# Attention sublayer of an encoder layer: gate and half of the second modulation summed in 1024-column pieces, in tiles of their own

## Chip, cores and metric

One core of one Trainium2 chip runs the whole layer as one program. The metric is the device time of one execution in microseconds (us); lower is better. PE is the matrix engine, PEld its weight loads, DVE the vector engine, ACT the scalar engine, POOL the general engine, SP the engine that here only issues DMAs. SPq is SP's queue of DMA issues, which runs in order.

## What is computed

One layer for a sequence of 512 rows of 2048 float32 values:

```python
mod = silu(c) @ w_ada + b_ada                     # 2048 x 12288 weights
sh1, sc1, gt1, sh2, sc2, gt2 = split(mod, 6)
h = rms_norm(x) * (1 + sc1) + sh1
mix = [differential attention(h), latent attention(h)] @ w_out
x = x + gt1 * mix
h2 = rms_norm(x) * (1 + sc2) + sh2
x = x + gt2 * ((silu(h2 @ w_gate) * (h2 @ w_up)) @ w_down)
```

Both attentions have 8 heads. c is one vector, so `silu(c) @ w_ada` is a vector times a matrix of 2048 rows. Those weights are read once and are not worth a matmul; DVE sums the products.

## The kernel before

**Matmuls.** float32 operands are split into a high part (ACT rounds, `hi`) and a low part (DVE or POOL subtracts, `lo`), and each product is three PE passes (`mm3`, lines 242 to 244). Class `Weights` loads a weight chunk into one of three `raw` tiles (lines 74 and 78, on SP), splits it (lines 90 and 98) and keeps two chunks ahead.

**A modulation sum.** `ada_sum` (line 299) sets 128 partitions to 16 rows of c each. For every q of the 16 it loads 128 rows by `width` columns of `w_ada` (line 308, SP) and DVE does acc = raw * c_col[q] + acc (line 315; the first one of a sum without a bias is a plain multiply, line 312). With a bias (line 303 and 304) POOL first clears acc and SP loads the bias into its first row. After 16 such steps the 128 partial rows are added up on PE by a product with ones. `ada_pair` (line 326) does the same for two parts at once: one tile holds `n` columns of the shift and `n` of the scale.

**Order of the work.** Only PE runs in the order in which the program is written. The order on each other engine is planned when the program is built, from its dependencies. In the attention the program is written as two hand-made lists of steps, one for a head of differential attention (`DIFF_STEPS`, nine `F`) and one for latent attention (`MLA_STEPS`, eight `F`, four of them `F1`). At each `F`, `between(us, n)` puts in `us` of projection matmuls as filler (`DIFF_FILL` and `MLA_FILL` per head; only 0.2 us for the fourth latent head) and then `n` steps of the generator `side_work`. `n` comes from `DIFF_SIDE[head]` and from `MLA_SIDE[0]` or `[1]`.

**Side work.** `side_work` first runs `gate1`: the 2048 columns of gt1, 512 at a time, by `ada_row` (line 359): 16 steps of one load and one sum, a step with the split of the sum (ACT and DVE), and a step with two matmuls by ones, a row copied out by DVE (line 953) and written to DRAM (line 954). That is 18 steps for each of 4 blocks. When the latent heads begin, `second_modulation` sums shift and scale of h2 for the first 8 of 16 column tiles (`MOD_EARLY`), 512 columns at a time by `ada_sums`: 32 sum steps, 6 empty ones and one with `ada_columns` (line 346, 16 small matmuls, line 354, and three DVE operations, lines 355 to 357) for each of 2 blocks. The other 8 column tiles are done later, in the output projection, and gt2 in the last stage; both by the same functions with other tiles.

**Tiles.** All loads and sums of the side work take slots of one ring `A` of 45 tiles of 512 columns (`slot_of`), which also holds the normed input, the latents, latent-attention keys and the attention's outputs. DMA scratch takes 16 KB of each partition in the build's default.

Of the kernel before, what the change touches and what calls it, by code (L numbers as in the profile page):

```python
# [10 lines left out]
F32 = mybir.dt.float32  # L11
F32R = mybir.dt.float32r
AF = mybir.ActivationFunctionType
ALU = mybir.AluOpType
# [4 lines left out]
P = 128  # L19
D = 2048  # L20
# [179 lines left out]
def hybrid_layer(ctx, tc, a, out):  # L200
    nc = tc.nc
    act, dve, pool, pe, sp = nc.scalar, nc.vector, nc.gpsimd, nc.tensor, nc.sync
# [9 lines left out]
    def open_pool(name, side="left"):  # L212
        p = tc.tile_pool(name=name, bufs=1, reuse_waits="tile", side=side)
        return p, p.__enter__()
# [8 lines left out]
    def slot(name, dt=F32R):  # L223
        return big.tile([P, S], dt, tag="A", bufs=N_SLOTS, name=name)

    def bank(tag, name):
        return psum.tile([P, 512], F32, tag=tag, name=name)

    turn, spare = [0], ["tmp"]

    def next_tag():
        turn[0] ^= 1
        return "tmp" if turn[0] else "acc"

    def f(ap):
        return ap.bitcast(F32)
# [17 lines left out]
    ones_r = const.tile([P, P], F32R, name="ones_r")  # L254
# [44 lines left out]
    def ada_sum(raws, accs, col0, width, nq, bias=None):  # L299

        acc = accs()
        if bias is not None:
            pool.memset(acc[:, :width], 0.0)
            sp.dma_start(out=acc[0:1, :width], in_=bias)
        for j in range(KC // nq):
            raw = raws()
            raw = raw[:, :nq * width].rearrange("p (q n) -> p q n", q=nq)
            sp.dma_start(out=raw, in_=w_ada[:, nq * j:nq * (j + 1), col0:col0 + width])
            for i in range(nq):
                q = nq * j + i  # L310
                if bias is None and q == 0:
                    dve.tensor_scalar(out=acc[:, :width], in0=raw[:, i, :width], scalar1=c_col[:, 0:1], scalar2=None,
                                      op0=ALU.mult)
                else:
                    dve.scalar_tensor_tensor(out=acc[:, :width], in0=raw[:, i, :width], scalar=c_col[:, q:q + 1],
                                             in1=acc[:, :width], op0=ALU.mult, op1=ALU.add)
            yield None
        yield acc

    def ada_sums(raws, accs, p_scale, p_shift, k0, nk, nq, sums):  # L320
        for part in (p_scale, p_shift):
            acc = None
            for acc in ada_sum(raws, accs, part * D + k0 * P, nk * P, nq):
                if acc is None:
                    yield None
            sums.append(acc)
# [21 lines left out]
    def ada_columns(sums, k0, nk, G, SH, cg, cbs, cbh):  # L348

        ks = slice(k0, k0 + nk)  # L350
        ps = bank(spare[0], "ps_ada")
        for i, acc in enumerate(sums):
            for m in range(nk):
                pe.matmul(ps[:, i * nk + m:i * nk + m + 1], acc[:, tsl(m)], ones, start=True, stop=True)
        dve.tensor_tensor(out=G[:, ks], in0=ps[:, 0:nk], in1=scol(cbs + k0, nk), op=ALU.add)
        dve.tensor_tensor(out=G[:, ks], in0=G[:, ks], in1=scol(cg + k0, nk), op=ALU.mult)
        dve.tensor_tensor(out=SH[:, ks], in0=ps[:, nk:2 * nk], in1=scol(cbh + k0, nk), op=ALU.add)

    def ada_row(raws, accs, part, c0, width, nq, tag, emit):

        acc = None
        col0 = part * D + c0
        for acc in ada_sum(raws, accs, col0, width, nq, b_ada[0:1, col0:col0 + width]):
            if acc is None:
                yield None
        ah, al = accs(F32R), accs(F32R)
        act.copy(out=ah[:, :width], in_=acc[:, :width])
        dve.tensor_tensor(out=al[:, :width], in0=acc[:, :width], in1=f(ah)[:, :width], op=ALU.subtract)
        yield None
        ps = bank(tag or spare[0], "ps_row")  # L370
        pe.matmul(ps[:, :width], ones_r, ah[:, :width], start=True, stop=False)
        pe.matmul(ps[:, :width], ones_r, al[:, :width], start=False, stop=True)
        emit(ps[:, :width], c0, width)
        yield None


    def raws0():
# [50 lines left out]
    ps = bank("tmp", "ps_small")  # L428
# [43 lines left out]
    k0, nk, _, _ = MODULATE[0]  # L472
# [112 lines left out]
    for i, (k0, nk) in enumerate(BLOCKS):  # L585
        final = i + 1 == len(BLOCKS)
        for h in range(1 if final else FIRST):
            tag = next_tag()
# [20 lines left out]
    wk = open_pool("wk")  # L609
# [337 lines left out]
    def slot_of(dt=F32):  # L947
        return slot("ada", dt)

    def gate1():  # L950
        def emit(ps, c0, width):
            row = slot_of()
            dve.tensor_copy(out=row[0:1, :width], in_=ps[0:1, :])
            sp.dma_start(out=rowd[0:1, c0:c0 + width], in_=row[0:1, :width])

        for c0 in range(0, D, 512):
            yield from ada_row(slot_of, slot_of, 2, c0, 512, 1, "tmp", emit)

    def out_half(b):

# [9 lines left out]
    def second_modulation(raws, accs, k0, k1, nq):  # L970
        for k in range(k0, k1, 4):
            sums = []
            yield from ada_sums(raws, accs, 4, 3, k, 4, nq, sums)
            for _ in range(6):
                yield None
            ada_columns(sums, k, 4, G2, SH2, C_G2, C_BSC2, C_BSH2)
            yield None
            G2_done[0] = k // 4 + 1
# [20 lines left out]
    def side_work():  # L999
        if GATE_EARLY:  # L1000
            yield from gate1()
        while 0 not in started:
            yield None
        if not GATE_EARLY:
            yield from gate1()
        yield from second_modulation(slot_of, slot_of, 0, MOD_EARLY, 1)

    half, G2_done = {}, [0]
    spare[0] = "tmp"
# [3 lines left out]
    def between(us, n):  # L1013
        fill.run(us)
        for _ in range(n):
            next(side, None)
# [9 lines left out]
    for h in range(H):  # L1026
        cur = diffs[h]
        for step in DIFF_STEPS.split():
            kind, i = step[0], int(step[1:] or 0)
            if kind == "F":  # L1030
                between(DIFF_FILL[h] / DIFF_STEPS.count("F"), DIFF_SIDE[h])
            elif kind == "n":
# [17 lines left out]
    for g in range(H + 1):  # L1050
# [4 lines left out]
        for step in MLA_STEPS.split():  # L1055
            kind, i = step[0], int(step[1:] or 0)
            if kind == "F":
                if g < H:
                    between(MLA_FILL[g] / MLA_STEPS.count("F"), MLA_SIDE[i])
            elif kind == "o":  # L1060
# [52 lines left out]
    def accs2(dt=F32):  # L1113
        return xtile("adaacc", dt)

    mod2 = second_modulation(xtile, accs2, MOD_EARLY, KC, 1)
    turn[0] = 1
    due = 0.0
    for b in range(4):
        tag = next_tag()  # L1120
# [265 lines left out]
    for u in range(N_UNITS):  # L1386
# [4 lines left out]
        else:  # L1391
# [4 lines left out]
                         in_=ao.rearrange("p (f c) s -> p f (c s)", f=2))  # L1396
# [3 lines left out]
    sums = [[fd[1].tile([P, 512], F32, tag="sums", bufs=16, name="sums") for _ in range(4)] for _ in range(NT)]  # L1400
# [26 lines left out]
    for i, n in enumerate(PARTS):  # L1427
        for b in range(4):
            tag = next_tag()
# [43 lines left out]
START_FILL = 5.2  # L1473
DIFF_STEPS = "s0 F s1 n F t0 F e s2 v0 F t1 F s3 v1 F t2 F o0 v2 t3 F o1 v3 F"
DIFF_FILL = (26.0, 26.0, 26.0, 26.0, 26.0, 26.0, 26.0, 26.3)
DIFF_SIDE = (1, 2, 1, 2, 1, 2, 1, 1)
MLA_SIDE = (1, 2)
MOD_EARLY = 8
MOD_PACE = (2.0, 2.4, 2.7, 1.5)
MLA_STEPS = "s0 F t0 e F1 t1 s1 v0 F t2 F1 v1 t3 s2 F v2 F1 o0 v3 F o2 o3 s3 o1 F1"  # L1480
# [39 lines left out]
```

## Time and profile before

| | us |
|---|---|
| three runs, median (lowest to highest) | 2257.24 (2250.57 to 2259.51) |
| profiled execution | 2254.27 |
| its span, first to last instruction | 2252.5 |
| granted TensorE clock, mean | 0.996 |

The profile lists how long each engine was busy, what it waited for, and which instructions it ran. Its windows give the busy time of each engine in a stretch of the span. The differential heads run from about 200 to 530 us, the latent ones from about 540 to 750 us; then come the output projection and, from about 890 us on, the feed-forward part.

### The profile page before, as it was taken

The page shows a single profiled execution, that of the slowest core. Times are in us where ns is not written, and L with a number is a line of the kernel's source. Part 1 is how long each engine was busy: PE and PEld are TensorE (multiplying, and loading weights), DVE is VectorE, ACT ScalarE, POOL GpSimd, SP SyncE. Part 2 cuts the span into 40 slices and gives each one's busy share as a digit, 9 for nine tenths or more (in the row PEclk, how much of TensorE's full clock was granted, in tenths as well). Part 3 has the DMA queues.
Part 4 walks back from the last instruction along what each step waited for, and adds up shares of the span by engine and source line. Part 5 has one row for each costly group of instructions (what it writes and reads, how often), then busy time and mean ns, then how long its engine had stood idle before and what let it go on. Part 6 is the DMA issues. An engine that isn't in the chain of part 4 may idle for free.

```text
span 2252.5 us, 35369 instructions
## 1 busy us (share of the span) xinstructions
PE 2178.6 (97%) x13906; PEld 2000.5 (89%) x13906; DVE 1648.1 (73%) x2362; ACT 942.6 (42%) x1567; POOL 262.7 (12%) x408
## 2 busy tenths in 40 slices
PE   3899999998989999999999999999999999999999
PEld 3899998998777788899999999999999888888887
DVE  5997888868988687867777777777777677443554
ACT  4434555566555334534444444444444522221221
POOL 0003444345554000000000000000000000000000
PEclk9999999999999999999999999999999999999999
DMA  9995355422442684523333333333334686333443
GB/s 284 302 292 169 83 154 158 134 87 86 158 139 96 247 295 159 159 85 118 117 118 117 132 122 122 114 118 116 122 123 131 219 296 224 99 127 99 154 149 103
DMA packets 270826, 345.00 MB, mean 153 GB/s; under 512 B 15005, under 2 KB 171142, under 8 KB 270530
## 3 DMA queue, kind: packets, MB, share of 16 engines
q1 hardware_dynamic: 267864, 338.18, 46.5%
q10 hardware_dynamic: 2794, 4.55, 0.5%
q8 instruction: 109, 1.79, 0.3%
q14 instruction: 59, 0.48, 0.1%
HBM read 322.71 MB, written 19.96 MB: 152 GB/s over the span
## 4 chain that ended last, share of the span: by engine, by line
PE 67%; DVE 1%; DMA 0%; ACT 0%; issue 0%; POOL 0%; SPq 0%; DVEq 0%
PE ps_d L243 7%; PE ps_d L244 7%; PE ps_d L242 7%; PE ps_X L1285 5%; PE ps_X L1283 5%; PE ps_X L1284 5%; PE ps_W L1285 3%; PE ps_W L1283 3%; PE ps_W L1284 3%; PE ps_Y L1285 2%; PE ps_Z L1285 2%; PE ps_o L242 2%; PE ps_o L244 2%; PE ps_o L243 2%; PE ps_Y L1283 2%; PE ps_Z L1283 2%
## 5 line engine op out<-in xcount | busy, mean ns | idle before, releaser
L90 ACT CAST hi<-raw 128x1024 fp32r<-128x1024 f32 (+2 forms) x228 | 221.2, 970 | 479.2 <-PE ps_d L243 262.7
L98 DVE TENSOR_TENSOR lo<-raw,hi 128x1024 fp32r<-128x1024 f32 (+2 forms) x215 | 242.6, 1129 | 217.3 <-ACT hi L90 213.5
L1266 ACT CAST wh<-wr 128x1024 fp32r<-128x1024 f32 x160 | 168.2, 1051 | 245.3 <-PE ps_X L1284 69.2
L1285 PE MATMUL ps_X<-comb,wl 128*128 128x256 f32 x960 | 269.4, 281 | 0.0
L1283 PE MATMUL ps_X<-comb,wh 128*128 128x256 f32 x960 | 268.6, 280 | 0.0
L1284 PE MATMUL ps_X<-comb,wh 128*128 128x256 f32 x960 | 267.1, 278 | 0.0
L1249 DVE TENSOR_TENSOR wl<-wr,wh 128x1024 fp32r<-128x1024 f32 x160 | 195.6, 1222 | 76.5 <-ACT wh L1266 76.2
L244 PE MATMUL ps_d<-lo,ax 128*128 128x512 f32 x640 | 249.0, 389 | 0.0
L243 PE MATMUL ps_d<-hi,ax 128*128 128x512 f32 x640 | 249.0, 389 | 0.0
L242 PE MATMUL ps_d<-hi,ax 128*128 128x512 f32 x640 | 249.0, 389 | 0.0
L242 PE MATMUL ps_in<-hi,hh 128*128 128x384 f32 (+2 forms) x704 | 234.9, 334 | 3.3 <-ACT hh L397 1.3
L243 PE MATMUL ps_in<-hi,hl 128*128 128x384 f32 (+2 forms) x704 | 229.2, 326 | 4.3 <-DVE hl L403 4.3
L244 PE MATMUL ps_in<-lo,hh 128*128 128x384 f32 (+2 forms) x704 | 229.2, 326 | 3.4 <-DVE lo L98 3.4
L1266 ACT CAST wh<-wt 128x1024 fp32r<-128x1024 f32 x120 | 126.4, 1053 | 196.0 <-PE ps_X L1284 118.5
L1249 DVE TENSOR_TENSOR wl<-wt,wh 128x1024 fp32r<-128x1024 f32 x120 | 146.7, 1223 | 80.5 <-ACT wh L1266 80.3
L1283 PEld LDWEIGHTS ps_X<-comb,wh 128*128 128x128 f32 x960 | 180.5, 188 | 0.0
L1284 PEld LDWEIGHTS ps_X<-comb,wh 128*128 128x128 f32 x960 | 180.5, 188 | 0.0
L1285 PEld LDWEIGHTS ps_X<-comb,wl 128*128 128x128 f32 x960 | 180.2, 188 | 0.0
L1285 PE MATMUL ps_W<-comb,wl 128*128 128x256 f32 x640 | 179.6, 281 | 0.0
L1283 PE MATMUL ps_W<-comb,wh 128*128 128x256 f32 x640 | 179.2, 280 | 0.0
L1284 PE MATMUL ps_W<-comb,wh 128*128 128x256 f32 x640 | 178.1, 278 | 0.0
L242 PEld LDWEIGHTS ps_d<-hi,ax 128*128 128x128 f32 x640 | 120.2, 188 | 25.0
(324 smaller groups left out, 5330.6 us busy)
## 6 DMA issues: line engine op xcount, KB each, us to landing
raw<-in_w_down_dram SPq DMA_DIRECT2D x88, 512.0 KB
araw<-in_w_ada_dram SPq DMA_DIRECT2D x80, 512.0 KB
wr<-in_w_gate_dram SPq DMA_DIRECT2D x40, 1024.0 KB
wr<-in_w_up_dram SPq DMA_DIRECT2D x40, 1024.0 KB
ada<-in_w_ada_dram SPq DMA_DIRECT2D x128, 256.0 KB
raw<-in_w_in_dram SPq DMA_DIRECT2D x128, 192.0 KB
raw<-in_w_out_dram SPq DMA_DIRECT2D x32, 512.0 KB
x<-in_w_ada_dram SPq DMA_DIRECT2D x64, 256.0 KB
```

The costliest lines, as they stand in the source:

```text
L90: nc.scalar.copy(out=hi[:, :n], in_=raw[:, :n])
L98: e.tensor_tensor(out=lo[:, :n], in0=raw[:, :n], in1=hi[:, :n].bitcast(F32), op=ALU.subtract)
L242: pe.matmul(o, ah, bh, start=start, stop=False)
L243: pe.matmul(o, al, bh, start=False, stop=False)
L244: pe.matmul(o, ah, bl, start=False, stop=stop)
L1249: dve.tensor_tensor(out=out, in0=x, in1=y, op=ALU.subtract)
L1266: act.copy(out=hi, in_=src)
L1283: pe.matmul(ps[bk], wh[:, k], c[:, 0], start=first and k == 0, stop=False, skip_group_check=True)
L1284: pe.matmul(ps[bk], wh[:, k], c[:, 1], start=False, stop=False, skip_group_check=True)
L1285: pe.matmul(ps[bk], wl[:, k], c[:, 0], start=False, stop=k == 7, skip_group_check=True)
```

## The change

gt1 is now summed 1024 columns at a time (2 blocks of 16 sums instead of 4) and the early second modulation with `ada_pair`, 512 columns of each of the two parts in one tile (2 blocks of 16 sums instead of 32). The loads go to two new tiles `sraw` and the sums to one new tile `sacc`, of 1024 columns each, in the attention's own pool. `ada_row` splits its sum 512 columns at a time; for the gate the split parts and the row stay slots of ring `A`. The steps at each `F` become one everywhere, none in the last differential head. The DMA scratch is set to 1 KB, which makes room for the 12 KB of new tiles.

```diff
-    def ada_row(raws, accs, part, c0, width, nq, tag, emit):
+    def ada_row(raws, accs, part, c0, width, nq, tag, emit, halves=None):
...
-        ah, al = accs(F32R), accs(F32R)
-        act.copy(out=ah[:, :width], in_=acc[:, :width])
-        dve.tensor_tensor(out=al[:, :width], in0=acc[:, :width], in1=f(ah)[:, :width], op=ALU.subtract)
-        yield None
-        ps = bank(tag or spare[0], "ps_row")
-        pe.matmul(ps[:, :width], ones_r, ah[:, :width], start=True, stop=False)
-        pe.matmul(ps[:, :width], ones_r, al[:, :width], start=False, stop=True)
-        emit(ps[:, :width], c0, width)
-        yield None
+        for i in range(0, width, 512):
+            part = acc[:, i:i + 512]
+            ah, al = [(halves or accs)(F32R)[:, :512] for _ in range(2)]
+            act.copy(out=ah, in_=part)
+            dve.tensor_tensor(out=al, in0=part, in1=f(ah), op=ALU.subtract)
+            yield None
+            ps = bank(tag or spare[0], "ps_row")
+            pe.matmul(ps, ones_r, ah, start=True, stop=False)
+            pe.matmul(ps, ones_r, al, start=False, stop=True)
+            emit(ps, c0 + i, 512)
+            yield None
...
+    def side_raw():
+        return wk[1].tile([P, 1024], F32, tag="sraw", bufs=2, name="sraw")
+
+    def side_acc():
+        return wk[1].tile([P, 1024], F32, tag="sacc", bufs=1, name="sacc")
...
-        for c0 in range(0, D, 512):
-            yield from ada_row(slot_of, slot_of, 2, c0, 512, 1, "tmp", emit)
+        for c0 in range(0, D, 1024):
+            yield from ada_row(side_raw, side_acc, 2, c0, 1024, 1, "tmp", emit, slot_of)
...
-            yield from ada_sums(raws, accs, 4, 3, k, 4, nq, sums)
+            if raws is side_raw:
+                yield from ada_pair(raws, accs, 4, 3, k, 4, sums)
+            else:
+                yield from ada_sums(raws, accs, 4, 3, k, 4, nq, sums)
...
-        yield from second_modulation(slot_of, slot_of, 0, MOD_EARLY, 1)
+        yield from second_modulation(side_raw, side_acc, 0, MOD_EARLY, 1)
...
-DIFF_SIDE = (1, 2, 1, 2, 1, 2, 1, 1)
-MLA_SIDE = (1, 2)
+DIFF_SIDE = (1, 1, 1, 1, 1, 1, 1, 0)
+MLA_SIDE = (1, 1)
...
-    nc = _bacc.Bacc("TRN2", target_bir_lowering=False, num_devices=1)
+    nc = _bacc.Bacc("TRN2", target_bir_lowering=False, num_devices=1, dynamic_dma_scratch_size=1024)
```

## Rows read from the trace of the kernel before

**Rows 1.** The page: span; busy us (share) xinstructions; GB/s in 40 slices.
```profile
span 2252.5 us, 35369 instructions
PE 2178.6 (97%) x13906; PEld 2000.5 (89%) x13906; DVE 1648.1 (73%) x2362; ACT 942.6 (42%) x1567; POOL 262.7 (12%) x408
...
GB/s 284 302 292 169 83 154 158 134 87 86 158 139 96 247 295 159 159 85 118 117 118 117 132 122 122 114 118 116 122 123 131 219 296 224 99 127 99 154 149 103
```

**Rows 2.** Windows: busy us of each engine (xinstructions) in each stretch, clock, DMA.
```profile
core 0: us, PE busy (x) PEld busy (x) DVE busy (x) ACT busy (x) POOL busy (x), PEclk, DMA share, GB/s
200.00:490.00 290.00, 284.30 (x1880) 274.62 (x1879) 240.10 (x504) 155.13 (x377) 126.10 (x189) 1.00 0.45 134
490.00:545.00 55.00, 47.74 (x278) 42.35 (x276) 42.68 (x94) 40.81 (x120) 39.71 (x91) 0.91 0.31 105
545.00:720.00 175.00, 164.47 (x835) 137.58 (x836) 156.49 (x297) 92.91 (x196) 89.29 (x116) 0.98 0.41 131
```

**Rows 3.** The same windows, only instructions on the tiles named ada.
```profile
200.00:490.00 290.00, 2.51 (x8) 1.40 (x8) 54.58 (x72) 2.48 (x4) 1.58 (x3) 1.00 0.45 134
545.00:720.00 175.00, 3.69 (x32) 3.79 (x32) 52.44 (x63) 0.00 (x0) 0.00 (x0) 0.98 0.41 131
```

**Rows 4.** Waits of PE, 200 to 490 us: us in total, times, longest us.
```profile
PE ps_z L759 <- DVE aTl L635: 2.8, 2, 2.2
PE ps_z L756 <- DVE aTl L635: 1.3, 1, 1.3
PE ps_in L244 <- DVE lo L98: 0.9, 2, 0.8
PE ps_in L242 <- DVE raw_s L532: 0.4, 1, 0.4
```

**Rows 5.** Waits of PE, 545 to 720 us, those on DVE.
```profile
PE ps_s L244 <- DVE kTl L638: 2.4, 3, 1.4
...
PE ps_aT L934 <- DVE pm L928: 1.6, 3, 0.5
PE ps_s L242 <- DVE SH L357: 1.6, 1, 1.6
PE ps_s L242 <- DVE q L635: 1.2, 1, 1.2
```

**Rows 6.** Groups of DVE by form, 0 to 190 us: xcount | busy us, mean ns | idle before.
```profile
L343 DVE SCALAR_TENSOR_TENSOR adaacc<-araw,c_col,adaacc 128x1024 f32<-128x1024 f32 x45 | 57.6, 1279 | 0.3
L341 DVE TENSOR_SCALAR adaacc<-araw,c_col 128x1024 f32<-128x1024 f32 x3 | 2.2, 748 | 0.0
```

**Rows 7.** Groups of DVE, whole span: the sums in the tiles named ada.
```profile
L315 DVE SCALAR_TENSOR_TENSOR ada<-ada,c_col 128x512 f32<-128x512 f32 x124 | 99.6, 803 | 11.6 <-DMA ada<-in_w_ada_dram 7.5 <-issue 3.0
L312 DVE TENSOR_SCALAR ada<-ada,c_col 128x512 f32<-128x512 f32 x4 | 2.3, 567 | 0.4 <-DMA ada<-in_w_ada_dram 0.4
```

**Rows 8.** The tiles named ada: duration ns min/median/max, first and last start us.
```profile
L308 SPq DMA_DIRECT2D ada<-in_w_ada_dram x128: 327/382/1499, 197.5 to 704.5; - x128
L315 DVE SCALAR_TENSOR_TENSOR ada<-ada,c_col x124: 724/748/2525, 205.3 to 708.8; 128x512 f32<-128x512 f32 x124
L303 POOL MEMSET ada<- x4: 524/526/528, 191.5 to 395.0; 128x512 f32 x4
L368 DVE TENSOR_TENSOR ada<-ada x4: 683/689/886, 284.7 to 450.9; 128x512 fp32r<-128x512 f32 x4
L953 DVE COPY ada<-ps_row x4: 669/670/679, 287.9 to 454.4; 1x512 f32<-1x512 f32 x4
```

**Rows 9.** Score matmuls of the differential (L727) and latent (L920) heads: duration, first and last start.
```profile
L727 PE MATMUL ps_s<-klo,q x64: 387/395/502, 227.3 to 530.4; 128*128 128x512 f32 x64
L920 PE MATMUL ps_s<-klo,q x32: 389/397/632, 543.3 to 746.6; 128*128 128x512 f32 x32
```

**Rows 10.** The chain that ended last, its two DMA pieces: start us, us, what.
```profile
698.20 3.57 DMA raw<-in_w_out_dram
...
704.53 4.27 DMA ada<-in_w_ada_dram
```

**Rows 11.** Waits of SP's queue, 540 to 720 us.
```profile
SPq L74 <- POOL lo L98: 75.2, 10, 15.3
SPq L308 <- PE ps_s L244: 12.3, 2, 10.8
...
SPq L308 <- DVE ada L315: 6.4, 6, 2.4
```

**Rows 12.** Timeline, 626 to 652 us: start, us, engine, line, operation [idle before <-releaser].
```profile
626.71 0.49 DVE L312 TENSOR_SCALAR ada<-ada,c_col 128x512 f32<-128x512 f32 x1 [0.40 <-DMA ada<-in_w_ada_dram]
...
630.82 0.16 DVE L355 TENSOR_TENSOR G<-ps_ada,small 128x4 f32<-128x4 f32 x1 [1.18 <-PE ps_ada L354]
...
647.95 0.75 DVE L315 SCALAR_TENSOR_TENSOR ada<-ada,c_col 128x512 f32<-128x512 f32 x1
...
648.69 0.74 DVE L638 SCALAR_TENSOR_TENSOR kTl<-ps_kT,small,kTh 128x512 fp32r<-128x512 f32 x1
...
649.49 0.59 PE L244 MATMUL ps_s<-kTl,qTh 128*128 128x512 f32 x1 [1.39 <-DVE kTl L638]
```

**Rows 13.** Windows: the stretch without filler.
```profile
626.00:652.00 26.00, 19.50 (x93) 15.10 (x92) 22.32 (x50) 11.83 (x27) 13.67 (x23) 0.89 0.33 104
```

## Prediction, written before the changed kernel was run

> **What bounds the kernel now.** I read the page first. PE is busy 2178.6 us of a span of 2252.5 us, so everything that any change can win without touching matmuls is the 74 us in which PE is idle; DVE is second with 1648.1 us [rows 1]. The changed code runs only in the attention, so I then cut the span into windows [rows 2]. Two of them hold side work: 200 to 490 us (gate), with PE idle for 290 - 284.30 = 5.7 us, and 545 to 720 us (second modulation), with PE idle for 175 - 164.47 = 10.5 us. There the granted clock is 0.98, so another 0.02 x 175 = 3.5 us of matmul pace is missing. The stretch between them, 490 to 545 us, has 7.3 us of idle PE, but DVE does no gate sum there, and I leave it out. **The most that can be won is 5.7 + 10.5 + 3.5 = 19.7 us**, 0.9% of the time.
>
> Who keeps PE waiting? In the waits of PE, DVE ended 2.8 + 1.3 + 0.9 + 0.4 = 5.4 us in the gate window [rows 4] and 2.4 + 1.6 + 1.6 + 1.2 = 6.8 us in the other [rows 5]. None of these tiles is a modulation sum: they are low parts, probabilities and projections that stood behind other work in DVE's queue. That is where a sum can do harm. The timeline shows one case: a sum starts at 647.95 us and takes 0.75 us, the low part of kT comes behind it at 648.69 us, and the matmul that reads it starts at 649.49 us after a wait of 1.39 us [rows 12]. DVE is busy 240.1 of 290 us and 156.5 of 175 us [rows 2], so in the second window there is little room to come late and catch up.
>
> **The change part by part.**
>
> *Sums on DVE.* Before there are 124 sums of 803 ns and 4 first products, 99.6 + 2.3 = 101.9 us [rows 7]. The same instruction on 1024 columns exists in the opening stage and takes 1279 ns, the first product 748 ns [rows 6]. The new work is 62 x 1.279 + 2 x 0.748 = 80.8 us. The opening stage has next to no POOL work beside it; in the attention the median of a 512-column sum is 748 ns, its mean 803 and its longest 2525 [rows 7, 8], so something stretches a few of them. If the stretch stays 55 ns per instruction it adds 3.4 us, if it stays whole 6.8 us, if it goes none. The saving is 14.3 to 21.1 us; I take the middle row, 17.7 us. By window: the gate has 54.58 us on these tiles, less four splits and four row copies of 0.69 and 0.67 us [rows 3, 8], so 49.1 us, and becomes 32 x 1.334 = 42.7 us, **6.4 us less**. The modulation has 52.4 us, and the first product that falls before the window makes it 52.9; it becomes 30 x 1.334 + 1.5 = 41.5 us, **11.4 us less**.
>
> *What of it reaches the end.* DVE is not on the path except where PE waits for it. As an estimate I let those waits shrink like busy over idle time of DVE, the usual growth of a queue. Modulation: 156.5/18.5 = 8.5 becomes 145.1/29.9 = 4.9, so 6.8 us of waits become 3.9, 2.9 us less; a like share of the idle time, 2.9/10.5, taken from the 3.5 us of clock is 1.0 us. Gate: 240.1/49.9 = 4.8 becomes 233.7/56.3 = 4.2, and 5.4 us become 4.7, 0.7 us less. Together **4.6 us less**. The bounds are nothing at all, if PE's next wait is on ACT just behind, and all 11.4 + 6.4 us, which the ceiling of 19.7 us just allows.
>
> *Pace.* A differential head takes 39 us (the last score row starts 303 us after the first, 31 of 32 score steps apart) and a latent one 26 us [rows 9]. The gate's 72 steps came 9 or 18 to a head and ended in head 5 (last row at 454.4 us [rows 8]); now its 40 steps come 9 to a head and end in head 4. DVE gets 11.5 us of sums in head 0 instead of 7.2, and 11.5 in a full later head instead of the 13.5 of a head with 18 steps. I cost this at nothing, because in head 0 the projection filler covers it; without the cover it would be 4.3 us. In the latent heads the rate hardly changes: 12 x 0.803 = 9.6 us per head before, 8 x 1.334 = 10.7 us after, but 46 steps instead of 78, so it ends three quarters of a head earlier. The stretch of 626 to 652 us, a head whose filler is nearly nothing, has DVE busy for 22.32 us and PE for 19.50 of 26 [rows 13]; there the new sums are longer by about 1 us, taken with the next item.
>
> *Single tile for the sum.* Before, DVE could start the next block's first product at 626.71 us, ahead of the last block's columns at 630.82 us [rows 12], in another slot. Now that product waits until PE has read the sum. The columns wait was 1.18 us; it stands in front of the scores on DVE, so I put 0.6 us on PE for it. At the gate's second block POOL's clear waits for the last split, which is two steps older; that is free. The clears themselves are two of twice the 526 ns [rows 8] and cost nothing on a POOL busy for 126 of 290 us [rows 2].
>
> *SP's queue.* 128 loads become 64 and four bias loads two; SP's 382 ns per issue [rows 8] hide behind waits. What SP waits for changes: now it stands 75.2 us for a weight tile that POOL splits, 12.3 us for a slot of ring `A` that the scores still read, and 6.4 us for a sum [rows 11]. The slot waits go away, because the ring is no longer used; a wait for the sum two steps back takes their place, with the weight loads queued behind it and the weight splits on ACT waiting for those. At one step per `F` the two steps are 26.2 / 8 x 2 = 6.6 us in a latent head and 8.7 us in a differential one. A 512 KB weight load took 3.57 us from issue to use and a 256 KB load of the sums, issued just behind one of those, 4.27 us [rows 10]. With 1.33 us for the sum in between, 4.9 to 5.6 us are needed of 6.6. I cost it at nothing on the mean, with the rival below as the other end.
>
> The Trainium skill, page "SBUF — State Buffer", section "The DMA setup-cost knee", says that each transfer pays a fixed part of roughly 2 us and then its bytes over 436 GB/s, so that fewer, larger transfers win. As an estimate from that page, a 512 KB load would take 3.2 us against 2.6 for 256 KB, the ring would turn in 4.5 us, and my sum would stand with more room. The rows are slower, 3.57 and 4.27 us [rows 10], and decide.
>
> *The rest.* PE's matmuls for rows and columns, ACT's casts and the row stores are the same in number and size. The later second modulation and gt2 run the same instructions as before. The DMA scratch is cut, but every load here is issued by SP or ACT, so I cost it at nothing.
>
> **Sum.** 4.6 - 0.6 = 4.0 us less. The profiled execution took 2254.27 us, its span 2252.5; it becomes 2250.3 us. It lies 3.0 us below the median of the three runs, 2257.24, so on that scale it is 2253.2. I give the middle, **2252 us**. About 0.5%, 11.3 us, is what a measurement of this kernel can tell from no change.
>
> **Rivals.**
>
> *A, DVE was the hidden bound, and the crowding ends.* All of DVE's waits and the lost clock go: 5.4 + 6.8 + 3.5 = 15.7 us, 2239 us. For it: DVE at 156.5 of 175 us, and sums directly ahead of late operands [rows 2, 12]. Against it: the rate of sums per latent head is the same, and a 1.28 us sum holds the queue longer than one of 0.75. Chance 0.23.
>
> *B, two load tiles are too few, slower.* Place: the latent heads. Price: the `F` steps are not evenly spaced, some `F` and `F1` have a single step between them. If half of the 32 loads come 1.0 us late, DVE stands still for 16 us with operands of PE behind the sum; where filler is short, DVE's delay is PE's [rows 13]. Less the 4 us won, it is 12 us more, 2266 us. It decides from the point where issue to use takes over 6.6 - 1.3 = 5.3 us; the 4.27 us row plus the additional 256 KB at the opening stage's 302 GB/s [rows 1] gives an estimate of 5.1 us, so it is close. Against it: the slots waited for now are as scarce [rows 11]. Chance 0.18.
>
> *C, nothing moves.* PE waits as long for other reasons, ACT or the chain of a head, and the planner's new order gives and takes a few us: 2254 us. Chance 0.17, inside no change.
>
> My forecast has 0.42.
>
> **How the numbers follow.** The forecast and C lie within 0.5%. Of A, a little falls short of 11.3 us; of B, a little too, and the forecast's own spread to both sides adds it back. Faster 0.24, same 0.57, slower 0.19. The range: the low end takes all 19.7 us, from the 2254.3 of the profiled run 2234.6, less 3.6 for runs that come out as low as the lowest of the three, 2231; the high end is B with its whole 16 us and nothing won, 2270.
>
> **What would show it.** Right: sums of about 1.28 to 1.34 us, 62 of them, DVE in 545 to 720 us down to about 145 us, PE's waits on DVE there at about 4 us, no slot wait for loads in SP's queue, loads landing before their sums. Wrong towards A: PE idle in both windows under 5 us and the clock at 1.00. Wrong towards B: DVE idle in front of the sums with the load as releaser, 10 us or more in total against 7.5 now [rows 7], SP waiting for the sums, and weight splits on ACT waiting for their loads. It would also be wrong if the projection or feed-forward stage changed its length by itself: I have given it nothing.

## Result: slower, and the profile after

The changed kernel takes 2272.07 us (median of 4 runs, 2271.76 to 2274.3) against 2256.43 us before (4 runs): a ratio of 1.0078, 95% interval [1.0064, 1.0092]. My forecast was 2252 us, my range ended at 2270. The interval lies clear of 1, so the change is slower, by 0.8%. The profiled execution took 2271.85 us, 17.6 us more than that of before.

The page of the profile after: span, then busy us (share) xinstructions of each engine.

```profile
span 2270.1 us, 35131 instructions
...
PE 2178.2 (96%) x13906; PEld 1998.5 (88%) x13906; DVE 1639.6 (72%) x2298; ACT 943.8 (42%) x1567; POOL 272.9 (12%) x406
```

Against [rows 1], DVE does have 8.5 us less to do, PE does the same, and all of the added span is idle PE. Windows after: busy us of each engine (xinstructions), clock, DMA share, GB/s.

```profile
200.00:490.00 290.00, 274.83 (x1786) 264.69 (x1785) 241.71 (x459) 148.48 (x360) 142.03 (x183) 0.98 0.52 158
490.00:545.00 55.00, 52.06 (x319) 47.17 (x319) 40.52 (x92) 40.47 (x116) 30.71 (x73) 0.97 0.24 73
545.00:720.00 175.00, 153.28 (x776) 128.96 (x775) 131.47 (x245) 88.42 (x194) 89.75 (x136) 0.93 0.27 85
640.00:680.00 40.00, 24.34 (x109) 18.73 (x108) 31.30 (x58) 13.10 (x29) 14.02 (x22) 0.79 0.50 151
```

PE idles for 15.2 us of the first window (5.7 before) and for 21.7 of the third (10.5 before) [rows 2]. The last row is a piece of the third: 15.7 us of it are idle in 40 us, at a clock of 0.79 (before, the same 40 us have 4.2 us of idle PE and a clock of 0.96). The tiles of the side work after (ns min/median/max, first and last start in us), and what DVE waited for in front of them:

```profile
L315 DVE SCALAR_TENSOR_TENSOR sacc<-sraw,c_col,sacc x32: 1264/1277/1716, 191.8 to 370.1; 128x1024 f32<-128x1024 f32 x32
L343 DVE SCALAR_TENSOR_TENSOR sacc<-sraw,c_col,sacc x30: 1262/1278/2675, 410.7 to 692.3; 128x1024 f32<-128x1024 f32 x30
L341 DVE TENSOR_SCALAR sacc<-sraw,c_col x2: 747/751/755, 409.9 to 634.8; 128x1024 f32<-128x1024 f32 x2
...
  DMA sraw<-in_w_ada_dram: 11.8, 11
```

The sums have the forecast duration and number. Their **places** don't. The gate starts at 191.8 us instead of 205.3 [rows 8]. The first modulation product comes at 409.9 us, where before the first of them came at 544.5 us, and 11 sums waited for loads, 11.8 us in all. The first products before:

```profile
L312 DVE TENSOR_SCALAR ada<-ada,c_col x4: 471/480/836, 544.5 to 668.6; 128x512 f32<-128x512 f32 x4
```

Waits of PE after, 200 to 490 us:

```profile
PE ps_z L761 <- DVE aTl L637: 4.3, 3, 2.1
PE ps_q L652 <- POOL qd L695: 4.2, 3, 1.8
PE ps_aT L751 <- DVE pm L742: 3.1, 2, 1.7
PE ps_z L758 <- DVE aTl L637: 2.5, 2, 1.8
```

and 545 to 760 us:

```profile
PE ps_k L652 <- POOL kpt L888: 12.1, 4, 9.1
```

DVE's part of the first list was 5.4 us [rows 4]; before, PE waited for POOL in these windows only once, 1.7 us, and for another tile. The score matmuls (first and last start) say how late the heads are:

```profile
L729 PE MATMUL ps_s<-klo,q x64: 387/394/398, 234.2 to 544.3; 128*128 128x512 f32 x64
L922 PE MATMUL ps_s<-klo,q x32: 387/397/628, 557.2 to 768.2; 128*128 128x512 f32 x32
```

Against [rows 9] the first differential score is 6.9 us late, the last 13.9, the last latent one 21.6. At the end of the span it is 17.6; where the other 4 us went is said below the table.

To see where each kernel loses, I took from its trace the time at which DVE starts its first pass over a head's scores, subtracted that of before, and list how much the delay grew over a stretch. D4 is differential head 4, M3 latent head 3 (the one without filler), both counted from 0. "Start" is the delay at D0, "later" the difference between M7's last score pair and the end of the span. All in us, from one profiled execution each.

| kernel | start | D0 to D4 | D4 to M3 | M3 to M4 | M4 to M7 | later | sum |
|---|---|---|---|---|---|---|---|
| after | 5.3 | -0.1 | 7.6 | 9.0 | -0.3 | -3.9 | 17.6 |
| e1_gate_only | 4.2 | -0.3 | 2.1 | -0.3 | 0.5 | 2.3 | 8.5 |
| e2_mod_only | 0.9 | 6.1 | -1.9 | 9.1 | -0.3 | -1.5 | 12.3 |
| e3_held | 6.3 | -1.4 | 9.2 | 8.1 | -0.9 | 3.0 | 24.3 |
| e4_scratch_only | 4.1 | 0.7 | 1.8 | 0.2 | 0.7 | -3.7 | 3.8 |
| e5_four_tiles | 4.0 | -3.2 | 1.0 | 6.8 | 1.0 | 2.0 | 11.5 |
| e6_skip_head3 | 3.6 | -1.2 | 8.2 | -1.7 | 7.5 | -4.5 | 11.8 |
| e7_own_512 | -1.1 | 2.5 | -1.9 | 0.1 | 1.6 | -3.1 | -1.9 |
| e8_half_sums | -0.2 | -5.1 | 6.5 | 5.6 | 4.3 | -3.8 | 7.3 |
| e9_one_load | 3.2 | -3.7 | 1.2 | 7.1 | 0.7 | -4.3 | 4.2 |
| e10_four_skip | 2.4 | -3.4 | 2.4 | 0.7 | 0.5 | -4.4 | -1.7 |
| e11_norm_first | 11.0 | -0.7 | 7.3 | 0.4 | 3.4 | -3.8 | 17.6 |
| e12_four_norm | 4.7 | -3.4 | 1.0 | 2.9 | 4.6 | -2.3 | 7.6 |
| e13_before_norm | -0.2 | 0.9 | 1.4 | -2.1 | 0.4 | -3.3 | -2.9 |
| e15_four_held | 3.9 | -3.6 | 3.1 | 7.8 | 1.5 | -1.4 | 11.3 |
| e16_four_held_norm | 3.8 | -3.2 | 2.8 | 2.9 | 1.8 | 1.7 | 9.8 |
| e17_gate_later | -0.7 | -2.7 | 0.7 | 1.2 | 0.3 | -1.4 | -2.5 |

How much of this is noise, e4 shows: it alters no side work and its median is that of before, yet its profile has 4.1 us at the start and -3.7 later. Windows of before and of e4, where the start differs, then of before and of after, where "later" arises:

```profile
40.00:100.00 60.00, 52.86 (x289) 49.97 (x290) 52.43 (x74) 26.65 (x46) 0.00 (x0) 1.00 0.94 303
40.00:100.00 60.00, 54.53 (x269) 51.97 (x270) 50.63 (x70) 23.76 (x41) 0.00 (x0) 0.90 0.93 296
1540.00:1720.00 180.00, 180.00 (x1530) 180.00 (x1530) 136.75 (x141) 78.92 (x96) 0.00 (x0) 1.00 0.36 119
1540.00:1720.00 180.00, 180.00 (x1545) 180.00 (x1545) 139.02 (x143) 79.31 (x97) 0.00 (x0) 1.00 0.37 123
```

e4 lost its 4 us in the opening stage, where the granted clock was 0.90 instead of 1.00. "Later" is PE's own pace in the feed-forward part, which no edit touches: at a granted clock of 1.00 and without a pause, PE got through 1530 or 1545 matmuls in 180 us. The 6720 matmuls of the gate and up products take 790.0 us before, 786.1 after and 785.5 to 793.1 in the other runs, and that is the "later" column to 0.3 us in each row. So the middle columns are good to 1 or 2 us, the first and the "later" one only to 4, and the medians decide on the sum. Each ratio below is against runs of the kernel before taken beside it (medians 2253.68 to 2256.43 us); where I compare two medians, I take the distance of each from its own before: 15.6 us for the changed kernel.

### The profile page after: what moved, and what is told of

It reads as the page before. It is cut to its first block, busy times and chain, and to the rows that moved or that the text cites. A ratio compares the mean times of both kernels' runs of the same rounds, so it can differ in the third digit from the quotient of the medians.

```text
span 2270.1 us, 35131 instructions
## 1 busy us (share of the span) xinstructions
PE 2178.2 (96%) x13906; PEld 1998.5 (88%) x13906; DVE 1639.6 (72%) x2298; ACT 943.8 (42%) x1567; POOL 272.9 (12%) x406
## 3 DMA queue, kind: packets, MB, share of 16 engines
q1 hardware_dynamic: 262740, 338.17, 46.1%
## 4 chain that ended last, share of the span: by engine, by line
PE 65%; DVE 3%; DMA 2%; ACT 0%; issue 0%; POOL 0%; DVEq 0%
PE ps_d L243 7%; PE ps_d L244 7%; PE ps_d L242 7%; PE ps_X L1294 5%; PE ps_X L1296 5%; PE ps_X L1295 5%; PE ps_W L1294 3%; PE ps_W L1296 3%; PE ps_W L1295 3%; PE ps_o L242 2%; PE ps_o L244 2%; PE ps_o L243 2%; PE ps_Z L1294 2%; PE ps_Y L1294 2%; PE ps_Y L1296 2%; PE ps_Z L1295 2%
```

## Experiments

**Halves of the change, and the scratch alone.** e1 keeps the gate of the change and gives the modulation back its slots, widths and pace; e2 the other way round.

```diff
 e1
-        yield from second_modulation(side_raw, side_acc, 0, MOD_EARLY, 1)
+        yield from second_modulation(slot_of, slot_of, 0, MOD_EARLY, 1)
-MLA_SIDE = (1, 1)
+MLA_SIDE = (1, 2)
 e2
-            yield from ada_row(side_raw, side_acc, 2, c0, 1024, 1, "tmp", emit, slot_of)
+            yield from ada_row(slot_of, slot_of, 2, c0, 512, 1, "tmp", emit)
-DIFF_SIDE = (1, 1, 1, 1, 1, 1, 1, 0)
+DIFF_SIDE = (1, 2, 1, 2, 1, 2, 1, 1)
 e4, on the kernel before
+    ... dynamic_dma_scratch_size=1024)
```

> Only the gate is changed; the early second modulation is summed as before, in 512-column slots of ring A, two steps at F1. Theory P (place of the sums): the loss is made by the modulation, whose first block of sums ran at 410 to 456 us, in differential heads 4 and 5, and whose second block filled the latent head without filler; both are gone here, the score of latent head 3 is no longer late, and only the 5 us that were lost by the first scores (235.2 against 229.9 us) stay: about 2259 us. Theory B (two load tiles are too few) looks at the latent heads too and gives much the same, 2256 to 2260. Theory S (the smaller DMA scratch, or the tiles' new addresses, cost by themselves) keeps the whole loss: about 2272.

Measured 2259.3 us, 1.0021 [1.0008, 1.0034].

> Only the early modulation is changed; the gate is summed as before. Theory P: the two new load tiles are free from the start of the attention, and nothing in the program holds the first block's 16 sums back, so the planned order puts them between the gate's in differential heads 0 and 1; the second block still falls into latent heads 3 and 4. Some 5 us lost at the start, 12 us in latent head 3: 2268 to 2275 us. Theory B: loads late in the latent heads, 2266. If the gate's change made the loss: 2256.

Measured 2271.48 us, 1.008 [1.0051, 1.011].

> The kernel before with the DMA scratch of 1 KB and nothing else. Theories P and B: no load uses the scratch, 2256 us. Theory S: up to 2272.

Measured 2255.07 us, 0.9998 [0.9985, 1.0011]. The scratch does nothing, the gate little, and the modulation alone is as slow as the whole change. (e2 also loses 6.1 us in D0 to D4, with the gate in the old slots. Its first modulation block runs there, from 189.3 to 285.3 us; I did not follow the waits.)

**Is it the loads?** Rival B had said two load tiles are too few. DVE's timeline after, and the PE matmul that waits, where the modulation's first block runs (start us, us; idle before in brackets):

```profile
410.71 1.28 DVE L343 SCALAR_TENSOR_TENSOR sacc<-sraw,c_col,sacc 128x1024 f32<-128x1024 f32 x1
...
415.30 1.28 DVE L343 SCALAR_TENSOR_TENSOR sacc<-sraw,c_col,sacc 128x1024 f32<-128x1024 f32 x1 [1.23 <-DMA sraw<-in_w_ada_dram]
...
427.42 1.28 DVE L343 SCALAR_TENSOR_TENSOR sacc<-sraw,c_col,sacc 128x1024 f32<-128x1024 f32 x1 [0.85 <-DMA sraw<-in_w_ada_dram]
...
431.35 1.28 DVE L343 SCALAR_TENSOR_TENSOR sacc<-sraw,c_col,sacc 128x1024 f32<-128x1024 f32 x1 [1.31 <-DMA sraw<-in_w_ada_dram]
432.55 0.68 DVE L637 TENSOR_TENSOR aTl<-ps_aT,aTh 128x512 fp32r<-128x512 f32 x1
...
433.29 0.66 PE L761 MATMUL ps_z<-v,aTl 128*128 128x128 f32 x4 [2.10 <-DVE aTl L637]
```

and SP's queue there:

```profile
410.70 8.03 SPq L337 DMA_DIRECT2D sraw<-in_w_ada_dram  x4
420.31 0.37 SPq L74 DMA_DIRECT2D raw<-in_w_in_dram  x1
...
422.69 0.37 SPq L337 DMA_DIRECT2D sraw<-in_w_ada_dram  x1
423.91 0.34 SPq L705 DMA_DIRECT2D strip<-vecd  x1
425.11 3.99 SPq L337 DMA_DIRECT2D sraw<-in_w_ada_dram  x2
```

The reader pairs them by the ring: a load goes out as soon as a sum has freed its tile and serves the sum after the next. Issued at 410.70, summed at 415.30; 422.69 and 427.42; 425.11 and 431.35: 4.60, 4.73 and 6.24 us, each with DVE waiting at its end. The block's 16 sums stand between 409.9 and 456.0 us, 46.1/15 = 3.1 us apart, so two steps less one sum leave 2 x 3.1 - 1.3 = 4.9 us. The operand aTl stands right behind such a sum at 432.55 us, and PE waits 2.10 us for it. By the page "SBUF — State Buffer" of the Trainium skill, section "The DMA setup-cost knee", my estimate for such a load was 3.2 us; these rows are 1.4 to 3.0 us above it.

Three kernels test it: e5 takes four load tiles (and three slots fewer in ring A), e9 leaves out 60 of the 64 loads (all sums of a block read the same columns), e8 sums only half of the columns.

```diff
 e5
-        return wk[1].tile([P, 1024], F32, tag="sraw", bufs=2, name="sraw")
+        return wk[1].tile([P, 1024], F32, tag="sraw", bufs=4, name="sraw")
-N_SLOTS = 45
+N_SLOTS = 42
 e9 (the same in ada_pair)
-            raw = raws()
+            if j == 0 or raws.__name__ != "side_raw":
+                raw = raws()
...
 e8 (the same in ada_pair)
-                    dve.scalar_tensor_tensor(out=acc[:, :width], in0=raw[:, i, :width], ...
+                    n = 512
+                    dve.scalar_tensor_tensor(out=acc[:, :n], in0=raw[:, i, :n], ...
```

> The changed kernel with four load tiles instead of two; ring A gives up three of its 45 slots for them. The planned order of DVE puts as many sums into each head as with two tiles, to one. Theory B: DVE's waits for sums' loads, 11.8 us, and SP's for sums, 49 us, mostly go, and the loss with them: 2256 to 2260 us. Theory P: the sums stand where they stood, waits for loads were short and mostly where DVE had nothing urgent: 2268 to 2273 us.

Measured 2265.12 us, 1.0044 [1.0028, 1.006].

> The changed kernel with one load for each block of 16 sums (the other 60 loads are left out; all sums of a block read that tile). The planned order of DVE puts as many sums into each head as in the changed kernel. If loads that come late and SP's queue behind them are the loss (theory B): 2255 to 2262 us. If DVE's time and the place of the sums are: 2267 to 2272, with the wait for the key's norm in latent head 3 still 10 us or more.

Measured 2256.64 us, 1.0018 [1.0006, 1.0031].

> The changed kernel with its loads and its order of sums, but each sum after a block's first adds only 512 of its 1024 columns (the other half of the sums is left out). DVE has 0.53 us less to do in each of 62 sums. If DVE's time is what was lost: 2256 to 2262 us, and the wait for the key's norm in latent head 3 under 7 us instead of 12.1. If it is the loads and the two tiles: 2268 to 2272.

Measured 2264.43 us, 1.0054 [1.0036, 1.0072]. What DVE waited for in front of the sums (us, times), in e5:

```profile
  DMA sraw<-in_w_ada_dram: 0.7, 1
```

The same of e9:

```profile
  DMA sraw<-in_w_ada_dram: 0.5, 1
```

And of e8:

```profile
  DMA sraw<-in_w_ada_dram: 21.5, 20
```

With four tiles or without the loads the wait is gone, and D0 to M3 falls from 7.5 us (-0.1 + 7.6) to -2.2 and -2.5: **two tiles cost about 10 us** up to there, nearly all of it in the differential heads. The first block, after and with four tiles:

```profile
L343 DVE SCALAR_TENSOR_TENSOR sacc<-sraw,c_col,sacc x15: 1262/1283/1523, 410.7 to 456.0; 128x1024 f32<-128x1024 f32 x15
L343 DVE SCALAR_TENSOR_TENSOR sacc<-sraw,c_col,sacc x15: 1262/1270/1522, 406.5 to 445.5; 128x1024 f32<-128x1024 f32 x15
```

With its first product at 405.7 us, e5's block takes 39.8 us instead of 46.1, its sums stand 2.65 us apart. That is the order unhindered, and it would leave a load in a ring of two only 2 x 2.65 - 1.28 = 4.0 us, less than any of the three took.

By the medians four tiles take off 5.2 us here (15.6 to 10.5), and in the pairs with one other edit below 8.6 (e11, e12), 9.3 (e6, e10) and 10.7 (e3, e15); so the price is 5 to 11 us. e9's median is 7.5 us nearer to its before than e5's, though both are about equally late at M7 (8.5 and 9.6 us); 6.3 us of that are "later", PE's pace in the profiled runs.

Halving the sums (e8) makes DVE wait longer for the same loads, but it too takes off a part: D0 to M3 is 1.4 us and M3 to M4 5.6, while M4 to M7 grows to 4.3, and by the median 4.9 us of the 15.6 go. So the length of the sums has a share in the loss, which these runs don't separate from the loads. And M3 to M4 stays at 6.8 and 7.1 us in e5 and e9, so there is a second cause.

**Is it the place of the first block?** e3 holds its first product on DVE behind the latest score reduction of the latent heads (`mark[0]`); e15 does that with four tiles.

```diff
+                    with tc.issue_after(mark[0]) if mark[0] and k0 == 0 else nullcontext():
+                        dve.tensor_scalar(out=acc, in0=raw[:, i], ...
```

> The changed kernel, with one edge more: the first product of the early modulation may not be placed on DVE ahead of the latest latent score reduction written before it. The first block's sums move back from differential heads 4 and 5 to latent heads 0 and 1. Theory P: the 6 us that heads 4 and 5 lost (scores 8 us late before, 14 us after) come back, the latent head without filler still loses its 10 to 13: 2263 to 2267 us. Theory B: more loads in the latent heads, where they come late: 2272 or more.

Measured 2276.18 us, 1.0094 [1.0066, 1.0122]: worse, not better.

> Four load tiles, with the first block of the early modulation held to the latent heads as in the run that held it with two tiles and lost 4 us more. If that run lost them because the two tiles are refilled too slowly for the quick steps of the latent heads: with four tiles as fast as four tiles alone, 2263 to 2267 us. If the latent heads have no room on DVE for these sums: 2268 or more.

Measured 2264.58 us, 1.0044 [1.0027, 1.0061]. The loss moves with the block: in e3, D4 to D5 alone falls from 8.7 to 1.2 us, but D5 to M3 rises from -1.1 to 8.0. With four tiles D4 to M3 is 1.0 us where the planner put the block and 3.1 us where I held it. So the early place by itself is no loss; it is one in a ring of two. e3 came out as theory B had said (2272 or more) and not as my theory P, that the place was the cause.

**The fourth latent head.** After's timeline of DVE and POOL in M3, and the matmul that waits:

```profile
653.07 1.28 DVE L343 SCALAR_TENSOR_TENSOR sacc<-sraw,c_col,sacc 128x1024 f32<-128x1024 f32 x1 [1.20 <-DMA sraw<-in_w_ada_dram]
...
655.32 1.28 DVE L343 SCALAR_TENSOR_TENSOR sacc<-sraw,c_col,sacc 128x1024 f32<-128x1024 f32 x1 [0.24 <-DMA sraw<-in_w_ada_dram]
...
657.31 0.41 DVE L874 TENSOR_REDUCE rsk<-sqm 128x2 f32<-128x256 f32 x1
...
657.80 0.20 POOL L882 TENSOR_TENSOR rsk<-rsk,sskpe 128x8 f32<-128x8 f32 x1 [11.33 <-DVE rsk L874]
...
660.94 0.61 POOL L888 TENSOR_TENSOR kpt<-kpe,rsk 128x256 f32<-128x256 f32 x1
...
661.60 0.47 PE L652 MATMUL ps_k<-ident,kpt 128*128 128x128 f32 x1 [9.11 <-POOL kpt L888]
```

Read it backwards: PE wants the rotated keys of the next pair of heads, POOL must first scale them by a norm, and the norm's last reduction (L874) stands on DVE behind six sums that started since 637 us, the last two of them shown. In the planned order of DVE before, all four reductions stand ahead of this head's scores; POOL scaled keys from 635.2 us on there, and PE did not wait for POOL. After, the last of them stand behind its third score tile. Before, the second block had begun at 626.71 us [rows 12]; here it starts at 634.8 us, when PE has read the single sum, and the planner packs its sums into this head. The late start is not what does it: with four tiles (e5) the block starts at 624.3 us, two of the four reductions still come at 643.3 and 644.1 us, behind this head's third score tile, and PE waits 6.8 us for the key.

e6 puts no steps into M3; e10 does that with four tiles.

```diff
-                    between(MLA_FILL[g] / MLA_STEPS.count("F"), MLA_SIDE[i])
+                    between(MLA_FILL[g] / MLA_STEPS.count("F"), 0 if g == 3 else MLA_SIDE[i])
```

> The changed kernel without side steps in latent head 3, the one without filler; the planned order has 2 sums there instead of 8, the others come in heads 4 and 5. Theory P: the wait of 9.1 us for the key's norm in that head goes, 8 to 12 us come back, the 6 us of differential heads 4 and 5 stay lost: 2260 to 2264 us. Theory B: the loads of heads 4 and 5 come as late as those of 3 did, 2266 to 2272.

Measured 2266.85 us, 1.0057 [1.0042, 1.0072].

> Both partial cures together: four load tiles and no side steps in latent head 3. Alone they gave back about 7 and 5 us of the 17, and the second left 6 us in latent head 5 behind a load that came 7.7 us late. If the causes are two, place and tiles: 2255 to 2260 us. If both removed the same loss: 2263 to 2267.

Measured 2256.59 us, 1.0012 [0.9998, 1.0026]. M3 to M4 falls to -1.7 and 0.7 us. With two tiles 7.5 us are lost again in M4 to M7, with four 0.5: with two, a load stands behind a weight load in SP's queue, as DVE's longest wait in e6 from 630 to 760 us and SP's queue show:

```profile
DVE sacc L343 <- DMA sraw<-in_w_ada_dram: 10.3, 2, 7.7
...
695.43 0.37 SPq L74 DMA_DIRECT2D raw<-in_w_out_dram  x1
695.89 7.28 SPq L337 DMA_DIRECT2D sraw<-in_w_ada_dram  x3
```

The sum that reads this load starts at 701.23 us. By the medians the edit takes off 3.4 us with two tiles and 7.5 with four.

e11, e12, e16 and e13 instead ask for the next pair's norms ahead of M3, on after, on e5, on e15 and on the kernel before.

```diff
+        if g == 3:
+            fill.until(lambda: 2 in pairs)
```

> The changed kernel, with the key's norm of the third pair written ahead of latent head 3 instead of in it. The planned order of DVE then has its four reductions ahead of that head's first score, as the kernel before had, and 7 sums in the head instead of 8. The two load tiles stay. Theory O (in latent head 3 it is only the planned order that costs: sums placed ahead of the key's norm): PE's wait for the key falls from 12.1 us to under 3, 8 to 12 us come back, 2260 to 2264 us, and the 8 us of the differential heads stay lost. If the sums themselves overload DVE in that head: 2268 to 2272.

Measured 2268.98 us, 1.0067 [1.0041, 1.0092].

> Four load tiles and the key's norm first. Theory: the two tiles cost the differential heads some 8 us, the planned order latent head 3 some 8 to 11; without both, 2250 to 2256 us, so no slower than the kernel before. If a third cause is left: 2258 or more.

Measured 2260.43 us, 1.0027 [1.0014, 1.004].

> Four load tiles, the modulation's first product held until the latent heads, and the key norms of the next pair asked for ahead of the fourth latent head: all three cures at once. Theory of separate places (tiles, place of the first block, fourth latent head): each cure works where it is put and they add up. From four tiles with the hold (2264.6 us) the norm should take off what it took off with four tiles alone, 4.7 us, so about 2260 us (2257 to 2262), with PE's wait for the rotated keys of the fourth latent head under 2 us. Rival, that all side work is now squeezed into the latent heads and DVE has too little idle time there: 2263 us or more, with the loss showing up in heads five and six in place of the fourth.

Measured 2262.59 us, 1.0033 [1.002, 1.0046].

> The kernel before with the key's norm written first. Its planned order had the four reductions ahead of the head's first score already; only one copy of the key moves ahead of some sums. Theory O: no difference, 2252 to 2257 us. If writing the norm earlier is a gain of its own, which would then not be the cure of the change: 2248 or less.

Measured 2251.3 us, 0.9985 [0.9971, 0.9999]: the one kernel whose interval lies below the kernel before, by about what can be told at all, and between my two expectations. Writing the norm first may thus be worth some 2.8 us by itself, without the change. PE's longest waits in e11 from 600 to 800 us:

```profile
PE ps_o L242 <- DVE kn L842: 2.5, 1, 2.5
PE ps_s L244 <- DVE kTl L640: 2.3, 1, 2.3
PE ps_z L243 <- DVE v L631: 2.2, 2, 1.5
```

The wait for kpt (12.1 us) is gone and M3 to M4 falls from 9.0 to 0.4 us, so the late norm was what stopped PE there. But small waits on DVE come in its place, M4 to M7 takes 3.4 us (4.6 in e12), and e11's median improves by only 1 to 3 us where I expected 8 to 12. The norm is the form of the loss; that sums crowded into a head without filler are its cause is the better reading, for taking them out of it (e10, 2.9 us above its before) keeps more of the gain than the norm first does (e12, 6.3). But those two intervals overlap, and no run separates what crowds the sums: their width, one step per `F`, or the single sum tile. e12 missed my 2250 to 2256 us and fell to "a third cause is left". It is 4.2 us better than e5 by the medians while M3 to M7 barely differ (7.5 against 7.8 us); the 2.8 us of e13 can be most of that. e16, without any wait for the key, came out above its range of 2257 to 2262 us, short of the rival's 2263, with 1.8 us lost in M4 to M7: the two cures did not add up as I expected, and why is open.

**Is it the width or the tiles?** e7 gives the kernel before its own tiles (four load tiles and two sums of 512 columns, scratch of 1 KB) at its old widths and pace.

```diff
+        return wk[1].tile([P, 512], F32, tag="sraw", bufs=4, name="sraw")
+        return wk[1].tile([P, 512], F32, tag="sacc", bufs=2, name="sacc")
```

> The kernel before, its 512-column sums and its pace, but with loads and sums in tiles of their own: four load tiles and two for the sums, 512 columns each. The planned order of DVE again pulls the modulation's first block forward, into differential heads 4 to 6 as far as 27 sums go, and leaves none in latent heads 0 to 2. Theory P alone (only the place of the sums counts): most of the loss is back, 2264 to 2270 us. Theory W (a sum that holds DVE for 1.28 us, with only two in reach, is what hurts in a bad place): 2255 to 2260 us.

Measured 2257.61 us, 1.0021 [1.0003, 1.0038]. Here too the gate and the first block moved forward (first sum at 190.4 us, first modulation product at 365.0), with no loss in D4 to M3 or M3 to M4, although DVE waited 10.8 us for these loads, nearly as long as after: what counts is not the total of that wait but what stands behind it. So own tiles alone are nearly free. e7 differs from the change in width, in steps per `F`, in the number of load tiles and in the second sum tile; only the number of load tiles was tried by itself.

**The start.** e17 is e10 with the gate's first sum held until the first head's square sums (`norm[0]`, the last of them so far) are done on DVE.

```diff
+                    with tc.issue_after(norm[0]) if norm[0] and q == 0 and col0 == 2 * D else nullcontext():
```

The timeline of POOL at the first head, in the changed kernel:

```profile
203.86 1.17 POOL L672 TENSOR_TENSOR qtab<-cs,gr 128x128 f32<-128x128 f32 x1
...
205.52 1.45 POOL L672 TENSOR_TENSOR qtab<-cs,gr 128x128 f32<-128x128 f32 x1
...
212.19 7.38 POOL L695 TENSOR_TENSOR qd<-raw_in,rs 128x256 f32<-128x256 f32 x8
```

The same in e17:

```profile
200.81 0.51 POOL L673 TENSOR_TENSOR qtab<-cs,gr 128x128 f32<-128x128 f32 x1
...
201.71 0.45 POOL L673 TENSOR_TENSOR qtab<-cs,gr 128x128 f32<-128x128 f32 x1
...
208.77 5.48 POOL L696 TENSOR_TENSOR qd<-raw_in,rs 128x256 f32<-128x256 f32 x8
```

> Four load tiles and no steps in the fourth latent head (2256.6 us), with one edit: the gate's first sum is held until the first head's square sums are done on DVE, so that the four gate sums that stood ahead of them in DVE's order stand behind them. Theory of the third place (gate sums that start at 192 us instead of 205 us delay the first head's norm on DVE and stretch POOL's work beside them, and PE waits 2.6 us for POOL's normed queries between 180 and 240 us): that wait goes, and the first score row comes 2 to 4 us earlier; the next heads give some of it back, so 2253 to 2256 us. Rival, that the wait has another cause (the ring of raw inputs, POOL's own pace): PE's wait for the queries stays over 2 us and the time stays at 2256 to 2258 us.

Measured 2254.58 us, 0.9996 [0.9983, 1.0009]. In e10 PE waited for qd, between 180 and 240 us:

```profile
PE ps_q L652 <- POOL qd L695: 2.2, 3, 0.9
PE ps_k L652 <- POOL qd L695: 0.4, 1, 0.4
```

In e17 no such wait is left and the first scores come 3.1 us earlier than in e10 (2.4 to -0.7). This is more than the noise of the start: from 200 to 240 us PE is busy for 37.4 us at a clock of 0.91 in e10, for 39.6 us at 1.00 in e17. The gate sums ahead of the first head's norm were a third, small cause.

## Why the prediction was wrong

- **Held:** 62 sums, 1277 ns in the median; with the first products they take 83.7 us instead of 101.9 [rows 7], 18.2 us less where I forecast 17.7 (DVE's whole busy time fell by 8.5 us; where the rest went I did not follow). The scratch is free, and no load waits any more for a slot that the scores read.
- **What was to be won is too small to be seen.** With the three waits repaired, e17 gains 1.2 us up to M7 in its profile, and its median equals that of before within 0.1%; the interval runs from 3.8 us less to 2.0 us more, and the forecast 4.0 lie just outside. The queue estimate that led to them is not shown. Rival A, DVE as the hidden bound with 15.7 us to win, is out.
- **The step that failed is "I cost it at nothing on the mean" for SP's queue.** I reckoned that two steps last 6.6 us in a latent and 8.7 us in a differential head, from the hand-written lists. But those lists fix only PE's order. The planner places DVE's and SP's work when it is ready: the 16 sums came 3.1 us apart, and 2.65 where no load held them up (e5). Two such steps less a sum are 4.0 us, against loads of 4.60 to 6.24 us: the ring is too short. Before, loads waited for slots of ring A, which scores and keys had to free. I saw those waits [rows 11] and counted their end as a gain; they were also a brake, as e7 shows: in tiles of their own, at the old widths and pace, the sums run ahead too. Rival B had the mechanism and about its price (16 us of waits less 4; measured about 10 by the profiles, 5 to 11 by the medians), but put it in the latent heads; most of it falls in the differential ones. I gave it 0.18.
- **"Pace ... I cost this at nothing" failed in the same way.** I reckoned with sums per head from the lists; the planner began the gate 13.5 us earlier, ahead of the first head's norm, and that cost 3.1 us by e17.
- **The stretch without filler** was put at "about 1 us" together with the single sum at 0.6 us. M3 to M4 grew by 9.0 us. I costed the longer sums, but not that the planner would put them in front of the norm of the next pair, and I didn't follow who waits for that: POOL, then PE.
- The three add to 10 + 3.1 and the 6.1 us by which skipping M3 helped with four tiles (6.8 to 0.7), 19.2 us of the 21.5 by which the attention is late at M7; the rest is within what one profile's start varies by. The medians agree: from after by e5 and e10 to e17 they fall by 5.2, 7.5 and 4.0 us, 16.7 in all, from 15.6 above the kernel before to 1.1 below.

Open: why PE's pace in the feed-forward part changes by 1%, e2's 6.1 us in the first heads, what crowds the sums into the fourth latent head, what share the length of the sums has (e8), and e16.

## What to carry to other kernels

When side work leaves a shared pool for tiles of its own, the waits for that pool go, and with them what held the work back: look up who decides its order, and reckon the ring against sums packed as densely as that order allows, not against the mean pace. Before pricing a longer instruction by its duration, look for the small operation behind it whose result another engine passes on to the bottleneck. A saving on an engine that isn't the bound is worth only the waits that it ends: 9.9 us less DVE work in e17 (1648.1 to 1638.2 us) bought nothing that can be measured here.

## What the hardware showed that I had not expected

POOL's 128x128 products of 0.45 to 0.51 us took 1.17 and 1.45 us when a DVE instruction with two inputs in SBUF ran at the same time: the low part at 203.49 us (1.22 us), and two sums at 205.16 us that themselves took 2.89 us instead of 2 x 1.28. In e17, where the sums stood later, the same products were undisturbed. There a small low part on DVE with two inputs in SBUF (v, 128x128, 0.28 us in the changed kernel) took 0.59 us beside a POOL product of 0.45, so DVE can be the one that pays. The Trainium skill, page "GPSIMD Engine Reference", section "Specifications", names this: POOL's way into SBUF is shared with DVE, with contention when DVE reads two SBUF inputs. The rows agree, at up to three times POOL's duration. Each sum reads two such inputs, so moving sums in front of POOL's work costs twice, by DVE's order and by the port.
